# Two of four weight-block sums by an adding transfer in a two-layer decoder trunk

## The chip, the cores and the metric

The kernel runs on one core of one Trainium2 chip. The metric is the device time of one execution, in microseconds. A core has five engines with instruction streams of their own: TensorE (PE; its weight loads are listed as PEld), VectorE (DVE), ScalarE (ACT), GpSimd (POOL) and SyncE (SP), which here only issues transfers.

## The reference

Two decoder layers on 256 tokens of width 2048, in float32. Layer 0 mixes tokens by multi-scale retention, layer 1 by latent attention; each mixer is followed by a SwiGLU block of width 5632, and every sub-layer is normed before and after:

```
for i in range(DEPTH):
    h = rms_norm(x, norm_mix_pre[i])
    h = retention(h, ...) if i % 2 == 0 else mla(h, ...)
    x = x + rms_norm(h, norm_mix_post[i])
    h = rms_norm(x, norm_ffn_pre[i])
    x = x + rms_norm(swiglu(h, ffn_w_gu[i], ffn_w_down[i]), norm_ffn_post[i])

def swiglu(x, w_gu, w_down):
    gate, up = jnp.split(x @ w_gu, [D_FF], axis=-1)
    return (jax.nn.silu(gate) * up) @ w_down
```

## The kernel before

Nearly all time goes into products of the 256 tokens (two tiles t of 128) with large weight matrices. A product is a `group`: it takes one slice of 1024 output columns and runs over the blocks kt of 128 rows of the weights. For each block, `weights` loads 128x1024 float32 from memory on SP's queue into a buffer `raw` (RAW = 4 of them), and `split` makes a high part in a rounded format on ScalarE (line 201) and a low part, the remainder, on VectorE (line 202), each into one of WB = 5 buffers. TensorE multiplies high by high, high by low and low by high: 12 matmuls of 512 columns for each block. `tile_load` issues the loads (line 415).

In some pairs of blocks the product of two by two blocks is made with 7 instead of 8 block products, in Winograd's form (`seven`): pairs p = 2 and 4 in the gate/up groups j = 1 to 10 of each SwiGLU (`GU_SEVENS`), and p = 2, 6, 10, 14, 18 in both halves of each down projection (`DN_SEVENS`). With b00, b01 the two halves of 512 columns of the pair's first block and b10, b11 those of its second, `right_sums` makes four sums of weight blocks:

- t1 = b00 + b01 and t3 = b01 + b11, side by side in the tile ta (lines 244, 245)
- t2 = t1 + b11 and t4 = t2 + b10, side by side in the tile tb (lines 246, 247)

Then ta and tb are split like any weights (tahi, talo, tbhi, tblo), each into one of the same 5 buffers; a pair thus takes 4 of them. ta and tb share 2 buffers (`tsum`). `left_sums` (lines 230 to 233) makes the sums of the activations. The products of a pair go in the order 1, 2, 3, 5, 7, 6, 4, where 5 and 7 read ta, and 6 and 4 read tb; in the last such pair of a group the order is 1, 6, 5, 7, 2, 3, 4, so that tb is read second. The first block of such a pair is loaded whole but only its first half is split (`first_half`); its second half b01 serves the sums alone.

Each engine runs its instructions in the order that a planner of the framework set when the kernel was built. It may put an instruction ahead of one that the program wrote earlier; on the chip an engine then waits at each instruction until its inputs are there, with all that is behind it. SP's transfers go out in order as well: a load waits until the raw buffer that it is to fill has been read by all its readers. The other names in the traces: gu and dn are the gate/up and down projections, m are the banks of products 1, 5, 6 and 7, b those of the result, sf, sh and sl the sums of activations and their parts, rvg, rqk, rto, mc, uq and mlo other products' weights.

Of the kernel before, what the change touches and what calls it, by code (L numbers as in the profile page):

```python
# [12 lines left out]
ALU = mybir.AluOpType  # L13
PSUM = bass.MemoryType.PSUM

P = 128
# [38 lines left out]
def trunk(  # L55
# [19 lines left out]
    nc = tc.nc  # L75
# [5 lines left out]
    def mm_bank(name):  # L81
        return ps.tile([P, 512], F32, tag="mm", bufs=6, name=name)
# [115 lines left out]
    def split(hi, lo, src, g=None):  # L198

        if g is None:  # L200
            nc.scalar.copy(out=hi, in_=src)  # L201
            nc.vector.tensor_sub(out=lo, in0=src, in1=hi.bitcast(F32))  # L202
        else:
            nc.scalar.activation(out=hi, in_=src, func=AF.Copy, scale=g)
            nc.vector.scalar_tensor_tensor(
                out=lo, in0=src, scalar=g, in1=hi.bitcast(F32), op0=ALU.mult, op1=ALU.subtract
            )
# [25 lines left out]
        nc.vector.tensor_add(out=sums[:, 3], in0=sums[:, 1], in1=a01)  # L233
        split(hi, lo, sums)

    def right_sums(raw0, raw1, name):

        b00, b01 = raw0[:, 0:512], raw0[:, 512:1024]
        b10, b11 = raw1[:, 0:512], raw1[:, 512:1024]
        res = {}  # L240
        ta = tp7.tile([P, 1024], F32, tag="tsum", bufs=2, name=f"{name}_ta")
        tb = tp7.tile([P, 1024], F32, tag="tsum", bufs=2, name=f"{name}_tb")
        t1, t3, t2, t4 = ta[:, 0:512], ta[:, 512:1024], tb[:, 0:512], tb[:, 512:1024]
        nc.vector.tensor_add(out=t1, in0=b00, in1=b01)
        nc.vector.tensor_add(out=t3, in0=b01, in1=b11)
        nc.vector.tensor_add(out=t2, in0=t1, in1=b11)
        nc.vector.tensor_add(out=t4, in0=t2, in1=b10)
        for both, src, n in ((ta, (1, 3), "a"), (tb, (2, 4), "b")):
            hi = wp.tile([P, 1024], F32R, tag="whi", bufs=WB, name=f"{name}_t{n}hi")
            lo = wp.tile([P, 1024], F32R, tag="wlo", bufs=WB, name=f"{name}_t{n}lo")  # L250
            split(hi, lo, both)
            for i, k in enumerate(src):
                sl = slice(i * 512, (i + 1) * 512)
                res[k] = hi[:, sl], lo[:, sl]
        return res

    def group(
        lhs, kts, load, name, lead=2, skew=0, tail=0, banks=None, between=None, sevens=(), left=None
    ):

# [5 lines left out]
        if banks is None:  # L266
            banks = [[mm_bank(f"{name}_b{t}{c}") for c in range(2)] for t in range(NT)]
        else:
            cols = banks[1]
            banks = banks[0]  # L270
        w = {}
# [30 lines left out]
            w[kt] = load(kt, True) if kt % 2 == 0 and kt // 2 in sevens else load(kt)  # L302

        def sums(p):
            w["t", p] = right_sums(w[2 * p][2], w[2 * p + 1][2], f"{name}_w{p}")

        def m_banks():
            for i, bank in ((1, mm_bank), (6, mm_bank), (5, misc_bank), (7, misc_bank)):
# [80 lines left out]
        for n, e in enumerate(plan):  # L389
# [15 lines left out]
    def tile_load(w, g, name, halves=0):  # L405

        def load(kt, first_half=False):
            n = 512 if kt < halves or first_half else 1024  # L410

            def dma(raw):
                for a in range(0, 1024, 512 if kt < halves else 1024):
                    m = 512 if kt < halves else 1024
                    nc.sync.dma_start(out=raw[:, a : a + m], in_=w[g, kt, :, a : a + m])

            parts = [(a, n, None) for a in range(0, 512 if first_half else 1024, n)]
            return weights(dma, parts, f"{name}_w{kt}")

        return load  # L420
# [55 lines left out]
    def closing(act, kts, w, g_post, col, name, skew=4, sevens=(), sums=None):  # L476
# [36 lines left out]
        for half in range(2):  # L513
            gp = sb.tile([P, 1024], F32, tag="gp", name=f"{name}_gp")
            nc.sync.dma_start(
                out=gp, in_=g_post[half * 1024 : (half + 1) * 1024].partition_broadcast(P)
# [44 lines left out]
            def first_done(banks):  # L561
# [9 lines left out]
            banks = group(  # L571
                lhs, kts, load, f"{name}{half}", skew=skew if half else 0, tail=2 if half else 0,
                between=first_done if half else None, sevens=sevens,
                left=lambda p, half=half: parts["s", half, p],
            )
            if half:
                stats(banks, 1)
# [191 lines left out]
    def swiglu(i):  # L769
        with tc.tile_pool(name=f"ff{i}", bufs=1) as fp:  # L770
# [32 lines left out]
            for j in range(FF // 512):  # L803
                name = f"gu{i}_{j}"
                banks = group(
                    h_lhs, DT, tile_load(w_gu[i], j, name), name, lead=2 if j else 4,
                    sevens=GU_SEVENS if 0 < j else (), left=lambda p: ins[p],
                )
# [289 lines left out]
    swiglu(0)  # L1098
    mla()
    swiglu(1)  # L1100


# [89 lines left out]
```

## Time and profile before

| what | value |
|---|---|
| median of 3 runs | 2454.28 us (2453.28 to 2454.59) |
| profiled execution, its time | 2454.15 us |
| its span, first to last instruction | 2452.3 us |
| busy: PE / PEld / DVE / ACT / POOL | 99% / 83% / 73% / 53% / 1% |
| moved by transfers | 463.75 MB, 189 GB/s |
| share of the 16 DMA engines, SP's queue | 57.1% |
| mean granted TensorE clock | 0.999 |

A row of the timeline gives start, duration, engine, line, operation, output<-inputs, shape and, in brackets, how long the engine was idle before it and what ended that. A row of groups gives the count, then busy microseconds and the mean nanoseconds of one, then the idle time before them with its releasers. A name that ends in q, as SPq, is an engine's queue of issues. Some hundredths of a microsecond between a releaser's end and the start of what it releases are normal. A low or high half in the text is the low or high part of a split, not half a block's columns.

### The profile page before, as it was taken

How to read it: one execution, taken by the hardware profiler on the slowest of the kernel's cores; microseconds unless marked ns; L12 is line 12 of the kernel's file. 1: busy time of each engine (PE TensorE's matmuls, PEld its weight loads, DVE VectorE, ACT ScalarE, POOL GpSimd, SP SyncE). 2: the span in 40 equal slices, each digit the busy share in tenths (PEclk: the TensorE clock that was granted, in tenths of full speed). 3: DMA queues.
4: the chain of work that ended last, by engine and by line, in shares of the span. 5: the costliest groups of instructions: out<-in, count | busy, mean ns of one | idle time of the engine just before them, and what ended most of it. 6: DMA issues, size and time to landing. Idle time of an engine off the chain costs nothing.

```text
span 2452.3 us, 30456 instructions
## 1 busy us (share of the span) xinstructions
PE 2438.9 (99%) x11128; PEld 2023.6 (83%) x11128; DVE 1799.4 (73%) x2379; ACT 1311.1 (53%) x1751; POOL 27.1 (1%) x38
## 2 busy tenths in 40 slices
PE   9999999999999999999999999999999999999998
PEld 7888888888888888888888888888888888888887
DVE  7655555555657787787888887876778777788887
ACT  5434544445545554555556666655555554556664
POOL 0000000000000000000000000000000000000000
PEclk9999999999999999999999999999999999999999
DMA  7555555555565566565656655445556656565664
GB/s 261 186 185 178 182 181 181 180 181 181 198 197 189 172 211 200 182 212 180 207 181 210 208 198 162 129 134 193 188 174 210 197 185 211 187 200 183 214 204 155
DMA packets 129607, 463.75 MB, mean 189 GB/s; under 512 B 14640, under 2 KB 15024, under 8 KB 129456
## 3 DMA queue, kind: packets, MB, share of 16 engines
q1 hardware_dynamic: 129456, 461.80, 57.1%
q8 instruction: 87, 1.43, 0.2%
q14 instruction: 64, 0.52, 0.1%
HBM read 459.64 MB, written 2.10 MB: 188 GB/s over the span
## 4 chain that ended last, share of the span: by engine, by line
PE 99%; DMA 0%; DVE 0%; SPq 0%; ACT 0%; issue 0%; DVEq 0%; POOL 0%; POOLq 0%; ACTq 0%
PE gu_b L398 34%; PE dn_b L398 17%; PE rvg_b L398 14%; PE rto_b L398 7%; PE rqk_b L398 7%; PE gu_m L398 4%; PE mlo_b L398 4%; PE q L398 3%; PE dn_m L398 2%; PE mc_b L398 2%; PE ftp L776 1%; PE ry L721 1%; PE htp L434 1%; PE asc L1032 0%; PE rsc L676 0%; PE asc L1029 0%
## 5 line engine op out<-in xcount | busy, mean ns | idle before, releaser
L398 PE MATMUL gu_b<-gu_w_hi,hT 128*128 128x512 f32 x2256 | 640.8, 392 | 0.0
L201 ACT CAST gu_w_hi<-gu_w_raw 128x1024 fp32r<-128x1024 f32 (+1 forms) x352 | 349.4, 1003 | 327.7 <-PE gu_b L398 252.3
L202 DVE TENSOR_TENSOR gu_w_lo<-gu_w_raw,gu_w_hi 128x1024 fp32r<-128x1024 f32 (+1 forms) x352 | 402.7, 1159 | 120.3 <-ACT gu_w_hi L201 120.0
L398 PEld LDWEIGHTS gu_b<-gu_w_hi,hT 128*128 128x128 f32 x2256 | 419.4, 188 | 85.7 <-DVE hT L202 0.9
L398 PE MATMUL gu_b<-gu_w_lo,hT 128*128 128x512 f32 x1128 | 358.2, 390 | 0.0
L398 PE MATMUL rvg_b<-rvg_w_hi,hT 128*128 128x512 f32 x1024 | 280.8, 391 | 0.0
L202 DVE TENSOR_TENSOR rvg_w_lo<-rvg_w_raw,rvg_w_hi 128x1024 fp32r<-128x1024 f32 x128 | 156.4, 1224 | 160.6 <-ACT rvg_w_hi L201 160.6
L398 PEld LDWEIGHTS gu_b<-gu_w_lo,hT 128*128 128x128 f32 x1128 | 211.5, 188 | 44.8 <-DVE gu_w_lo L202 0.6
L201 ACT CAST rvg_w_hi<-rvg_w_raw 128x1024 fp32r<-128x1024 f32 x128 | 134.7, 1053 | 195.8 <-PE rvg_b L398 187.4
L201 ACT CAST dn_w_hi<-dn_w_raw 128x1024 fp32r<-128x1024 f32 (+1 forms) x176 | 174.3, 1003 | 104.1 <-PE dn_b L398 55.9
L398 PEld LDWEIGHTS rvg_b<-rvg_w_hi,hT 128*128 128x128 f32 x1024 | 191.1, 188 | 38.9
L202 DVE TENSOR_TENSOR dn_w_lo<-dn_w_raw,dn_w_hi 128x1024 fp32r<-128x1024 f32 (+1 forms) x176 | 200.0, 1160 | 23.6 <-ACT dn_w_hi L201 22.9
L398 PE MATMUL dn_b<-dn_w_hi,dn_ah 128*128 128x512 f32 x564 | 178.2, 390 | 0.0
L398 PE MATMUL dn_b<-dn_w_lo,dn_ah 128*128 128x512 f32 x564 | 178.0, 390 | 0.0
L398 PE MATMUL dn_b<-dn_w_hi,dn_al 128*128 128x512 f32 x564 | 178.0, 390 | 0.0
L398 PE MATMUL rvg_b<-rvg_w_lo,hT 128*128 128x512 f32 x512 | 158.1, 390 | 0.0
L398 PE MATMUL rqk_b<-rqk_w_hi,hT 128*128 128x512 f32 x512 | 141.0, 393 | 2.0 <-ACT hT L201 1.0
L398 PEld LDWEIGHTS dn_b<-dn_w_lo,dn_ah 128*128 128x128 f32 x564 | 105.9, 188 | 22.0
L398 PEld LDWEIGHTS dn_b<-dn_w_hi,dn_al 128*128 128x128 f32 x564 | 105.9, 188 | 21.9
L398 PEld LDWEIGHTS dn_b<-dn_w_hi,dn_ah 128*128 128x128 f32 x564 | 105.6, 188 | 21.6
L202 DVE TENSOR_TENSOR rqk_w_lo<-rqk_w_raw,rqk_w_hi 128x1024 fp32r<-128x1024 f32 (+1 forms) x65 | 77.5, 1207 | 59.3 <-ACT rqk_w_hi L201 59.3
L201 ACT CAST rqk_w_hi<-rqk_w_raw 128x1024 fp32r<-128x1024 f32 (+1 forms) x65 | 67.4, 1038 | 99.4 <-PE rqk_b L398 90.2
(307 smaller groups left out, 3851.6 us busy)
## 6 DMA issues: line engine op xcount, KB each, us to landing
gu_w_raw<-w_gu SPq DMA_DIRECT2D x352, 512.0 KB, 4.3
dn_w_raw<-w_down SPq DMA_DIRECT2D x176, 512.0 KB, 4.4
rvg_w_raw<-ret_vg SPq DMA_DIRECT2D x128, 512.0 KB, 3.5
rto_w_raw<-ret_out SPq DMA_DIRECT2D x64, 512.0 KB, 3.5
rqk_w_raw<-ret_qk SPq DMA_DIRECT2D x63, 512.0 KB, 4.0
mlo_w_raw<-mla_out SPq DMA_DIRECT2D x32, 512.0 KB, 3.5
uq_w_raw<-mla_up SPq DMA_DIRECT2D x32, 448.0 KB, 3.4
mc_w_raw<-mla_c SPq DMA_DIRECT2D x16, 512.0 KB, 4.6
```

The source lines that it names most:

```text
L201: nc.scalar.copy(out=hi, in_=src)
L202: nc.vector.tensor_sub(out=lo, in0=src, in1=hi.bitcast(F32))
L398: nc.tensor.matmul(out, e[2](), e[3](), start=bank not in begun, stop=ends[bank, bank in added] == n, skip_group_check=bank in added,)
L434: nc.tensor.transpose(tp[:, j * P : (j + 1) * P], xs[:, t, (k0 + j) * P : (k0 + j + 1) * P], ident)
L721: nc.tensor.matmul(y, left, right, start=n == 0, stop=n == len(terms) - 1)
L776: nc.tensor.transpose(tp[:, b * P : (b + 1) * P], a[:, b * P : (b + 1) * P], ident)
```

## The change

Of a pair's first block only the first half is loaded into its raw buffer. ScalarE copies b00 into t1's place and b11 into t3's place in ta. Then one transfer, issued by GpSimd, reads b01 from memory twice (a source repeated over two rows) and adds it to both halves of ta. t2 and t4 stay adds on VectorE.

```
-        nc.vector.tensor_add(out=t1, in0=b00, in1=b01)
-        nc.vector.tensor_add(out=t3, in0=b01, in1=b11)
+        nc.scalar.copy(out=t1, in_=b00)
+        nc.scalar.copy(out=t3, in_=b11)
+        nc.gpsimd.dma_start(
+            out=ta.rearrange("p (i c) -> p i c", i=2),
+            in_=b01_again[:, None, :].to_broadcast([P, 2, 512]), accum_op=ALU.add,
+        )
         nc.vector.tensor_add(out=t2, in0=t1, in1=b11)
         nc.vector.tensor_add(out=t4, in0=t2, in1=b10)
...
-                for a in range(0, 1024, 512 if kt < halves else 1024):
-                    m = 512 if kt < halves else 1024
-                    nc.sync.dma_start(out=raw[:, a : a + m], in_=w[g, kt, :, a : a + m])
+                for a in range(0, 512 if first_half else 1024, n):
+                    nc.sync.dma_start(out=raw[:, a : a + n], in_=w[g, kt, :, a : a + n])
```

The argument `b01_again` is the slice `[..., 512:1024]` of the weights in memory, handed down through a new parameter `second_half` of `group`; in the down projection it is `w[half, kt, :, 512:1024]`, in gate/up `w_gu[i][j, kt, :, 512:1024]`.

More of the change, by code (lines that the diff above doesn't have):

```diff
@@ L234, in left_sums, with right_sums @@
         split(hi, lo, sums)
-    def right_sums(raw0, raw1, name):
-        b00, b01 = raw0[:, 0:512], raw0[:, 512:1024]
+    def right_sums(raw0, raw1, b01_again, name):
+        b00 = raw0[:, 0:512]
         b10, b11 = raw1[:, 0:512], raw1[:, 512:1024]
@@ L257, in group @@
     def group(
-        lhs, kts, load, name, lead=2, skew=0, tail=0, banks=None, between=None, sevens=(), left=None
+        lhs, kts, load, name, lead=2, skew=0, tail=0, banks=None, between=None, sevens=(), left=None,
+        second_half=None,
     ):
@@ L304, in sums @@
         def sums(p):
-            w["t", p] = right_sums(w[2 * p][2], w[2 * p + 1][2], f"{name}_w{p}")
+            w["t", p] = right_sums(w[2 * p][2], w[2 * p + 1][2], second_half(2 * p), f"{name}_w{p}")
         def m_banks():
@@ L574, in closing @@
                 left=lambda p, half=half: parts["s", half, p],
+                second_half=lambda kt, half=half: w[half, kt, :, 512:1024],
             )
@@ L807, in swiglu @@
                     sevens=GU_SEVENS if 0 < j else (), left=lambda p: ins[p],
+                    second_half=lambda kt, j=j: w_gu[i][j, kt, :, 512:1024],
                 )
```

## The prediction

> **What bounds the kernel now.** I read the page's busy times first, then the chain that ended last, then a window over everything but the first 12 us and the last ones. The first row is the page's, the second its chain, the third the window (length, then busy time and count of PE, PEld, DVE, ACT, POOL, then granted clock, DMA share, GB/s).
>
> ```profile
> PE 2438.9 (99%) x11128; PEld 2023.6 (83%) x11128; DVE 1799.4 (73%) x2379; ACT 1311.1 (53%) x1751; POOL 27.1 (1%) x38
> ...
> PE 99%; DMA 0%; DVE 0%; SPq 0%; ACT 0%; issue 0%; DVEq 0%; POOL 0%; POOLq 0%; ACTq 0%
> ...
> 12.00:2440.00 2428.00, 2427.32 (x11084) 2016.98 (x11083) 1788.07 (x2356) 1303.04 (x1731) 26.31 (x33) 1.00 0.57 189
> ```
>
> TensorE is the bound and nothing else is: in 2428.00 us it is idle for 0.68 us, at full clock. VectorE's 1788 us in that window lie wholly beside it. So work taken off VectorE can give at most 0.68 us; the change alters no matrix product, so it can only leave the time alone or cost time. Everything turns on whether the sums of weight blocks still arrive before TensorE asks for them.
>
> **The change part by part.** It touches right_sums, which runs 60 times: 40 times in the gate/up groups and 20 times in the down projection. The adds that go:
>
> ```profile
> L245 DVE TENSOR_TENSOR gu_w_ta<-gu_w_raw 128x512 f32<-128x512 f32 x40 | 27.6, 690 | 32.2 <-DMA gu_w_raw<-w_gu 32.2
> L244 DVE TENSOR_TENSOR gu_w_ta<-gu_w_raw 128x512 f32<-128x512 f32 x40 | 27.6, 690 | 4.7 <-DMA gu_w_raw<-w_gu 4.0
> L245 DVE TENSOR_TENSOR dn_w_ta<-dn_w_raw 128x512 f32<-128x512 f32 x20 | 13.7, 686 | 0.0
> L244 DVE TENSOR_TENSOR dn_w_ta<-dn_w_raw 128x512 f32<-128x512 f32 x20 | 13.7, 685 | 0.0
> ...
> L777 ACT COPY aT<-ftp 128x512 f32<-128x512 f32 x44 | 25.5, 579 | 0.0
> ```
>
> Removed from VectorE: 27.6 + 27.6 + 13.7 + 13.7 = 82.6 us, worth nothing by the window above. Added on ScalarE: 2 copies of 128x512 in each of 60 places at the 0.579 us of the last row (that one reads PSUM; it is the nearest), 120 x 0.579 = 69.5 us, hidden under its idle 47% as long as they are not late themselves.
>
> Added as transfers: 60 on GpSimd's queue, each writing 512 KB and reading 256 KB of weights twice; 60 loads on SP's queue shrink from 512 to 256 KB. Net 60 x 256 KB = 15.7 MB on the 463.75 MB of the page, 3.4%. The page's first row counts 38 instructions on GpSimd in the whole kernel, so next to nothing queues behind the new wait there. SP's queue is another matter, below.
>
> The price that no row shows is L: from the end of the second copy to the landed sum. The nearest rows are SP's plain loads (KB, then median us from issue to landing) and GpSimd's small operations (count, busy us, mean ns):
>
> ```profile
> gu_w_raw<-w_gu SPq DMA_DIRECT2D x352, 512.0 KB, 4.3
> dn_w_raw<-w_down SPq DMA_DIRECT2D x176, 512.0 KB, 4.4
> ...
> cst<-consts SPq DMA_DIRECT2D x1, 64.0 KB, 1.9
> ...
> L118 POOL TENSOR_TENSOR grs<-bve,mhalf 128x1 f32<-128x1 f32 x16 | 8.8, 548 | 550.8 <-DVE bve L727 550.8
> L118 POOL TENSOR_TENSOR rto_x_r<-rto_x_v,mhalf 128x1 f32<-128x1 f32 x2 | 4.2, 2096 | 24.0 <-DVE rto_x_s L451 23.7 <-DVE rto_x_v L453 0.3
> ```
>
> Lower end: 4.3 us, if the transfer costs what a plain load of its size does. Upper end: it must also read its 512 KB target before it can add, and GpSimd issues it instead of SP; two loads in a row and the longest GpSimd row give 2 x 4.3 + 2.1 = 10.7 us. Between: the 64 KB row puts the part that does not grow at about 1.9 us, so 512 KB move in 2.4 us; twice that, plus 1.9, plus 0.55 for GpSimd, is 6.85. The GpSimd part is nearer to its 0.55 than to 2.1, but the new transfer also shares 16 engines that are busy 57% of the time, so I take L = 7.2 us, an estimate.
>
> The Trainium skill bears on the doubling: "Collectives: The Full Stack", section "The bandwidth ceiling", says that a transfer that adds sends two reads for each chunk through the same ring and so runs at half the rate of a copy. No row here shows an adding transfer; by that rule alone the sum would be the one I take.
>
> Now where L lies. These are the rows of one gate/up group's two sums (block pairs 2 and 4), VectorE first, then TensorE:
>
> ```profile
> 929.24 0.68 DVE L245 TENSOR_TENSOR gu_w_ta<-gu_w_raw 128x512 f32<-128x512 f32 x1
> ...
> 933.81 1.23 DVE L202 TENSOR_TENSOR gu_w_lo<-gu_w_raw,gu_w_hi 128x1024 fp32r<-128x1024 f32 x1 [1.29 <-ACT gu_w_hi L201]
> ...
> 938.50 0.69 DVE L245 TENSOR_TENSOR gu_w_ta<-gu_w_raw 128x512 f32<-128x512 f32 x1 [1.33 <-DMA gu_w_raw<-w_gu]
> 939.11 1.22 DVE L202 TENSOR_TENSOR gu_w_tblo<-gu_w_tb,gu_w_tbhi 128x1024 fp32r<-128x1024 f32 x1
> ...
> 940.45 0.68 DVE L246 TENSOR_TENSOR gu_w_tb<-gu_w_ta,gu_w_raw 128x512 f32<-128x512 f32 x1
> ...
> 941.25 0.68 DVE L247 TENSOR_TENSOR gu_w_tb<-gu_w_tb,gu_w_raw 128x512 f32<-128x512 f32 x1
> 941.85 2.95 DVE L202 TENSOR_TENSOR gu_w_lo<-gu_w_raw,gu_w_hi 128x1024 fp32r<-128x1024 f32 x3
> ...
> 947.95 1.05 ACT L201 CAST gu_w_tbhi<-gu_w_tb 128x1024 fp32r<-128x1024 f32 x1 [1.66 <-PE gu_b L398]
> ...
> 949.03 1.23 DVE L202 TENSOR_TENSOR gu_w_tblo<-gu_w_tb,gu_w_tbhi 128x1024 fp32r<-128x1024 f32 x1 [1.49 <-ACT gu_w_tbhi L201]
> ...
> 943.90 0.39 PE L398 MATMUL gu_m<-gu_w_tblo,sh 128*128 128x512 f32 x1
> 945.49 0.39 PE L398 MATMUL gu_b<-gu_w_lo,hT 128*128 128x512 f32 x1
> ...
> 951.38 0.39 PE L398 MATMUL gu_m<-gu_w_tblo,sh 128*128 128x512 f32 x1
> ```
>
> After the landed transfer, the rest of the chain is two adds (941.25 + 0.68 - 940.45 = 1.48 us), the high half on ScalarE (1.05) and the low half on VectorE (1.22): 3.75 us.
>
> First sum of the group: its second block is there at 929.24. Copy 0.58, L, 3.75: the low half is ready at 933.57 + L, and TensorE reads it at 943.90. Hidden up to L = 10.3.
>
> Second sum: hidden cover is shorter, because the first one now delays its load. The raw buffer of the first sum's second block was freed by the low half that ends at 933.81 + 1.23 = 935.04. Now the two late adds read that buffer too, and end at 929.24 + 0.58 + L + 1.48 = 931.30 + L. With 4 raw buffers, the load four blocks on (the second block of the second sum, landed at 938.50) waits for just this buffer, on SP's in-order queue, as it did before:
>
> ```profile
> SPq L415 <- DVE gu_w_lo L202: 789.7, 341, 8.1
> ```
>
> It therefore lands L - 3.74 later, at 934.76 + L. Copy 0.58, L again, 3.75: ready at 939.09 + 2L, wanted at 951.38. It is in time up to L = 6.14; beyond that TensorE stops for 2L - 12.29. At L = 7.2 that is 2.1 us, in 20 groups (10 of each layer's 11) 42 us.
>
> In the down projection two sums are further apart, and the load four blocks on is no sum's. An ordinary place and the last of a half:
>
> ```profile
> 2234.49 0.69 DVE L245 TENSOR_TENSOR dn_w_ta<-dn_w_raw 128x512 f32<-128x512 f32 x1
> 2246.55 0.39 PE L398 MATMUL dn_m<-dn_w_tblo,sh 128*128 128x512 f32 x1
> ...
> 2297.61 0.69 DVE L245 TENSOR_TENSOR dn_w_ta<-dn_w_raw 128x512 f32<-128x512 f32 x1
> ...
> 2307.07 0.39 PE L398 MATMUL dn_m<-dn_w_tblo,sh 128*128 128x512 f32 x1
> ```
>
> Ordinary: 12.06 - 0.58 - 3.75, hidden up to 7.7. Last: 9.46 - 4.33, hidden up to 5.1, so 2.1 us at L = 7.2, four times (two halves, two layers): 8 us.
>
> Sum: 42 + 8 = 50 us on the profiled execution's own 2454.15 us, which stands 0.1 us under the median of the runs: 2504 us. At 8.6 (two loads in a row) it is 20 x 4.9 + 4 x 3.5 + 16 x 0.9 = 126 us, 2580; at 10.7 about 2700; at 4.3 nothing.
>
> **The rivals.**
> Hidden anyway (the other side: not slower). If L stays under 5.1 us every sum is in time by the above, and 2454 us stays; between 5.1 and 6.1 only the four last sums are late, at most 4 us in all. For it: the plain loads' 4.3 us. Against it: the second read and GpSimd's part. The Trainium skill, "DMA: Bandwidth & Descriptors", section "Anatomy of one DMA", gives about 2.0 us plus bytes over 436 GB/s for a transfer issued by GpSimd; with 512 KB that is 3.2 us and with the target's read counted too 4.4 us, both estimates, and by either the time stays 2454 us. No run here shows it yet.
>
> The order on VectorE. Its instructions start in a planned order, not when they are ready. The row at 939.11 shows it: its high half was long cast, and it stood behind the add that waited 1.33 us for a load. If the plan puts the add that needs the transfer (as now, 940.45) ahead of the three low halves of 941.85, they stand behind it. TensorE reads the first of them at 945.49. At L = 4.3 the load lands 0.56 us later, the transfer at 939.06 + 0.58 + 4.3 = 943.94, two adds and one low half end at 946.64: 1.15 us late, 23 us over 20 groups, 2477 us, although L itself would be hidden. At 7.2 it is 1.15 + 2 x 2.9 = 6.95 us, 139 us, 2593. Against it: a plan that reckons with a late transfer sets those halves first.
>
> A transfer much slower than two loads (over 8.6 us): beyond 2580 us. Only the upper end of L speaks for it.
>
> **How the numbers follow.** Forecast, L between 6.1 and 8.6 with the order adapted: 0.36. Hidden: 0.34. Order: 0.19. Slower transfer: 0.09. Faster: 0.02, since the window leaves 0.68 us and 0.2% (5 us, about what a measurement tells from no change) is needed. Same gets the hidden case and the forecast's edge, 0.35; slower 0.63. The likeliest case gives 2504 us, with its own range 2459 to 2580. The range 2453 to 2600 takes in the hidden case at one end and most of the order's at the other; the slower transfer and the rest of the order's case, about 0.15, lie outside.
>
> **What would show it.** Right: VectorE's busy time falls by about 80 us, ScalarE's rises by about 70, and TensorE has gaps of some 2 us, 20 of them at the product that reads the gate/up sums' second pair and 4 at the down projection's last, released by VectorE's low half or ScalarE's high half of tb; the transfers take about 7 us from issue to landing. Wrong by size: landing in 5 us or less and TensorE still without gaps. Wrong by place: gaps at the ordinary low halves, with VectorE idle in front of the add that makes t2.

## The result and the profile after

The changed kernel takes 2671.71 us (median of 4, 2665.79 to 2676.48) beside 2454.41 us for the kernel before on the same chip: a ratio of 1.0885, 95% interval 1.0862 to 1.0908, 217 us more. The prediction had the sign and the place of the gate/up stops; it gave 2504 us, 50 us more, with a range to 2600, so the loss is four times the forecast and outside the range.

The page of the changed kernel: busy times, chain, GpSimd's queue (packets, MB, share of 16 engines' span) and its two groups of transfers (count, KB each, median us from issue to landing).

```profile
PE 2536.1 (95%) x11128; PEld 2063.5 (77%) x11128; DVE 1723.8 (64%) x2259; ACT 1360.4 (51%) x1871; POOL 100.1 (4%) x98
...
q0 software_dynamic: 16320, 31.46, 7.3%
...
PE 62%; DMA 19%; DVE 10%; issue 4%; ACT 4%; SPq 0%; DVEq 0%; ACTq 0%; POOL 0%; POOLq 0%
...
gu_w_ta<-w_gu POOLq DMA_DIRECT2D x40, 512.0 KB, 6.4
dn_w_ta<-w_down POOLq DMA_DIRECT2D x20, 512.0 KB, 9.3
```

A chain that was 99% TensorE is now 62%, with 19% transfers and 10% VectorE. VectorE's 75.6 us less and ScalarE's 49.3 us more go the way of the moved work (the copies' records overlap their neighbours', so their 120 x 0.62 us do not add up in full). The loss is in the first row: the span grew by 222.1 us (2452.3 to 2674.4); TensorE's idle time grew from 13.4 to 138.3 us, and its busy time by 97.2 us for the same 11128 matmuls. These are two losses of different kinds.

The idle time, by groups (idle before them and its releaser last in the row):

```profile
L405 PE MATMUL gu_m<-gu_w_tbhi,sh 128*128 128x512 f32 x40 | 18.7, 467 | 43.1 <-ACT gu_w_tbhi L201 43.1
L405 PE MATMUL gu_m<-gu_w_tblo,sh 128*128 128x512 f32 x40 | 21.6, 541 | 16.7 <-DVE gu_w_tblo L202 16.7
L405 PE MATMUL dn_b<-dn_w_lo,dn_ah 128*128 128x512 f32 x564 | 182.1, 397 | 32.9 <-DVE dn_w_lo L202 32.9
L405 PE MATMUL dn_m<-dn_w_tbhi,sh 128*128 128x512 f32 x20 | 9.9, 496 | 15.9 <-ACT dn_w_tbhi L201 15.9
L405 PE MATMUL dn_m<-dn_w_tblo,sh 128*128 128x512 f32 x20 | 10.5, 527 | 5.5 <-DVE dn_w_tblo L202 5.5
L405 PE MATMUL dn_m<-dn_w_talo,sh 128*128 128x512 f32 x40 | 22.2, 556 | 4.8 <-DVE dn_w_talo L202 4.8
```

Gate/up stops almost only where a product reads tb (43.1 + 16.7 = 59.8 us; 3.8 us stand at ordinary low halves). In the down projection a little more than half, 32.9 us, stands at ordinary low halves, which are made from no sum; the last three rows, 26.2 us, are products that read sums.

The busy time, by windows over the two gate/up stages (first and third row) and the two down projections (length, then PE, PEld, DVE, ACT, POOL busy and count, granted clock, DMA share, GB/s); the last row is a stretch of 3.3 us right after one gate/up stop:

```profile
753.00:1291.00 538.00, 506.31 (x2159) 408.10 (x2157) 358.11 (x420) 275.75 (x347) 29.10 (x23) 0.96 0.61 184
1291.00:1575.00 284.00, 252.90 (x1038) 201.38 (x1037) 183.85 (x238) 148.65 (x212) 12.70 (x11) 0.94 0.59 175
1845.00:2386.00 541.00, 507.02 (x2160) 406.65 (x2159) 357.75 (x418) 276.91 (x345) 29.31 (x24) 0.96 0.61 184
2386.00:2668.00 282.00, 250.60 (x1024) 199.37 (x1022) 181.01 (x231) 142.27 (x190) 12.71 (x12) 0.94 0.56 166
...
1020.80:1024.10 3.30, 3.30 (x9) 2.52 (x9) 2.63 (x3) 0.79 (x1) 0.00 (x0) 0.50 0.49 178
```

The granted clock, 1.00 before, is 0.96 and 0.94: after most stops it is 0.50 for 3.4 or 6.8 us. Summed over the four stages that is 160 us at half clock, so up to 80 us of the 97.2 (the matmuls that began at half clock make up some 70 us of it). Most of the rest are the first matmuls behind a stop: they count with their whole record, where in a stream the records overlap.

One gate/up group, its two sums, in order of time:

```profile
995.29 0.62 ACT L246 COPY gu_w_ta<-gu_w_raw 128x512 f32<-128x512 f32 x1
...
1002.14 0.69 DVE L251 TENSOR_TENSOR gu_w_tb<-gu_w_ta,gu_w_raw 128x512 f32<-128x512 f32 x1 [5.87 <-DMA gu_w_ta<-w_gu]
1002.75 1.22 DVE L202 TENSOR_TENSOR gu_w_lo<-gu_w_raw,gu_w_hi 128x1024 fp32r<-128x1024 f32 x1
1003.88 0.69 DVE L252 TENSOR_TENSOR gu_w_tb<-gu_w_tb,gu_w_raw 128x512 f32<-128x512 f32 x1
...
1008.13 0.62 ACT L246 COPY gu_w_ta<-gu_w_raw 128x512 f32<-128x512 f32 x1 [0.34 <-DMA gu_w_raw<-w_gu]
1009.16 1.20 POOL L247 DMA_DIRECT2D gu_w_ta<-w_gu  x1 [11.62 <-ACT gu_w_ta L246]
1015.63 0.69 DVE L251 TENSOR_TENSOR gu_w_tb<-gu_w_ta,gu_w_raw 128x512 f32<-128x512 f32 x1 [2.93 <-issue]
1016.24 1.22 DVE L202 TENSOR_TENSOR gu_w_lo<-gu_w_raw,gu_w_hi 128x1024 fp32r<-128x1024 f32 x1
1017.37 0.69 DVE L252 TENSOR_TENSOR gu_w_tb<-gu_w_tb,gu_w_raw 128x512 f32<-128x512 f32 x1
...
1018.17 1.05 ACT L201 CAST gu_w_tbhi<-gu_w_tb 128x1024 fp32r<-128x1024 f32 x1 [1.46 <-DVE gu_w_tb L252]
1019.24 1.23 DVE L202 TENSOR_TENSOR gu_w_tblo<-gu_w_tb,gu_w_tbhi 128x1024 fp32r<-128x1024 f32 x1
1019.26 0.50 PE L405 MATMUL gu_m<-gu_w_tbhi,sh 128*128 128x512 f32 x1 [2.17 <-ACT gu_w_tbhi L201]
1020.52 0.60 PE L405 MATMUL gu_m<-gu_w_tblo,sh 128*128 128x512 f32 x1 [0.76 <-DVE gu_w_tblo L202]
```

From the start of the last copy to t2 the first sum takes 6.85 us, the second 7.50; a low half (the second and the fifth VectorE row) stands between t2 and t4 in both. (The L of the tables below counts from GpSimd's issue, which begins some 0.4 us after the copy's end: 995.91 to 996.33 in this group.) Between the two sums lies a load that lands 3.5 us after the first t4 ends. SP's queue waited for those adds; its waits (total us, times, longest):

```profile
SPq L421 <- DVE gu_w_tb L252: 254.6, 38, 9.8
...
SPq L421 <- DVE dn_w_tb L252: 203.0, 20, 11.8
```

In the kernel before, the same two waits are next to nothing:

```profile
SPq L415 <- DVE dn_w_tb L247: 5.1, 2, 2.6
...
SPq L415 <- DVE gu_w_tb L247: 0.8, 1, 0.8
```

An ordinary place of the down projection:

```profile
1378.29 0.69 DVE L251 TENSOR_TENSOR dn_w_tb<-dn_w_ta,dn_w_raw 128x512 f32<-128x512 f32 x1 [8.01 <-DMA dn_w_ta<-w_down]
1378.90 1.22 DVE L202 TENSOR_TENSOR dn_w_lo<-dn_w_raw,dn_w_hi 128x1024 fp32r<-128x1024 f32 x1
...
1380.17 0.80 PE L405 MATMUL dn_b<-dn_w_lo,dn_ah 128*128 128x512 f32 x1 [3.23 <-DVE dn_w_lo L202]
```

VectorE waits 8.01 us at t2 for the transfer; behind it stands a low half that needs nothing of the sum, and TensorE needs that half.

### The profile page after: what moved, and what is told of

Its sections match the earlier page's. It is cut to its first block, busy times and chain, and to the rows that moved or that the text cites. A ratio compares the mean times of both kernels' runs of the same rounds, so it can differ in the third digit from the quotient of the medians.

```text
span 2674.4 us, 30714 instructions
## 1 busy us (share of the span) xinstructions
PE 2536.1 (95%) x11128; PEld 2063.5 (77%) x11128; DVE 1723.8 (64%) x2259; ACT 1360.4 (51%) x1871; POOL 100.1 (4%) x98
## 4 chain that ended last, share of the span: by engine, by line
PE 62%; DMA 19%; DVE 10%; issue 4%; ACT 4%; SPq 0%; DVEq 0%; ACTq 0%; POOL 0%; POOLq 0%
PE gu_b L405 18%; PE rvg_b L405 13%; DMA gu_w_ta<-w_gu 8%; PE rto_b L405 7%; PE rqk_b L405 6%; DMA dn_w_ta<-w_down 6%; PE mlo_b L405 3%; PE dn_b L405 3%; PE q L405 3%; DMA dn_w_raw<-w_down 3%; PE gu_m L405 3%; DVE dn_w_lo L202 2%; DMA gu_w_raw<-w_gu 2%; DVE gu_w_lo L202 2%; PE mc_b L405 2%
## 5 line engine op out<-in xcount | busy, mean ns | idle before, releaser
L201 ACT CAST gu_w_hi<-gu_w_raw 128x1024 fp32r<-128x1024 f32 (+1 forms) x352 | 343.0, 1001 | 285.5 <-PE gu_b L405 226.1
L405 PE MATMUL dn_b<-dn_w_lo,dn_ah 128*128 128x512 f32 x564 | 182.1, 397 | 32.9 <-DVE dn_w_lo L202 32.9
L251 DVE TENSOR_TENSOR gu_w_tb<-gu_w_ta,gu_w_raw 128x512 f32<-128x512 f32 x40 | 27.7, 693 | 184.2 <-DMA gu_w_ta<-w_gu 139.3
```

The source lines that it names most:

```text
L405: nc.tensor.matmul(out, e[2](), e[3](), start=bank not in begun, stop=ends[bank, bank in added] == n, skip_group_check=bank in added,)
```

## The experiments

In the table, the times are medians in us, each beside the kernel before on the same chip; the stages are the spans of the two gate/up stages and the two down projections in the profiled run; L is the median us from issue to landing of the transfers in gate/up and in the down projection.

| kernel | time | ratio, 95% interval | gate/up | down | L |
|---|---|---|---|---|---|
| before | 2454.4 | | 478.2, 478.2 | 234.3, 233.3 | |
| after | 2671.71 | 1.0885 (1.0862 to 1.0908) | 538.6, 541.0 | 284.1, 282.5 | 6.4, 9.3 |
| filled stop | 2633.26 | 1.0738 (1.0704 to 1.0772) | 521.0, 521.9 | 280.8, 281.2 | 6.2, 9.1 |
| no wait | 2459.30 | 1.0024 (1.0014 to 1.0033) | 480.8, 479.9 | 234.4, 233.3 | 7.0, 9.8 |
| t2, t4 on GpSimd | 2727.28 | 1.1115 (1.1098 to 1.1131) | 554.3, 564.2 | 288.6, 289.4 | 6.4, 9.0 |
| half the transfer | 2492.57 | 1.0157 (1.0142 to 1.0172) | 486.4, 486.9 | 248.6, 240.8 | 4.4, 7.2 |
| t2 behind the low half | 2718.52 | 1.1085 (1.1060 to 1.1109) | 572.0, 568.3 | 275.6, 272.3 | 8.1, 9.1 |
| writing, by GpSimd | 2516.15 | 1.0253 (1.0229 to 1.0277) | 484.4, 484.9 | 255.7, 253.5 | 4.5, 6.2 |
| writing, by ScalarE | 2503.37 | 1.0201 (1.0184 to 1.0218) | 494.4, 499.4 | 239.7, 240.1 | 4.5, 6.1 |
| five raw buffers | 2670.99 | 1.0878 (1.0860 to 1.0895) | 545.5, 551.6 | 270.8, 272.7 | 7.2, 9.5 |
| gate/up pairs 2 and 5 | 2662.27 | 1.0842 (1.0827 to 1.0857) | 540.3, 536.0 | 280.8, 277.4 | 6.8, 8.9 |
| second sum only | 2557.09 | 1.0417 (1.0401 to 1.0433) | 480.8, 479.4 | 283.8, 280.6 | 6.4, 9.2 |
| first sum only | 2617.19 | 1.0668 (1.0638 to 1.0697) | 518.8, 513.5 | 285.1, 281.6 | 8.0, 9.2 |
| split behind t4 | 2672.39 | 1.0877 (1.0859 to 1.0895) | 542.5, 533.5 | 285.1, 282.8 | 6.4, 9.3 |

The theories by their letters: A, the half clock is caused by the stops; B, the wait costs and not the added work; C, VectorE's order makes the down projection's stops; D, the length L sets the stops; E, adding is dearer than writing; F, the first sum holds its raw buffer and so delays the second; G, what adding costs when nothing shares the engines; H, the low half between t2 and t4.

**A, the clock.** Twelve matmuls of zeros fill the stop in front of product 6 of a group's last pair:

```
+    FILL = 12
...
+                if final and i == 6:
+                    plan.append(("do", fill))
                 product(*m[i])
...
+        def fill():
+            for _ in range(FILL):
+                nc.tensor.matmul(ms[6], zeros, zeros[:, None, :].to_broadcast([P, 4, P]), start=False, stop=False)
```

> The changed kernel with 12 matmuls of zeros (about 0.22 us each) put ahead of product 6 of the last pair of each group, so that TensorE works while it waits for tb. Theory A: a part of the loss is TensorE's clock, which the profile of the changed kernel shows at 0.5 for 3.4 or 6.8 us behind each longer stop (47.8 and 44.4 us in the two gate/up stages, of which half is lost: 46 us). With TensorE kept busy the half-clock stretches in gate/up go, the stop stays as long as the zero matmuls: about 2672 - 46 = 2626 us. Rival: the clock record costs nothing, or follows something else than the stop: the time stays within 8 us of the changed kernel's 2672.

The first gate/up stage of that kernel:

```profile
753.00:1274.00 521.00, 512.32 (x2281) 403.90 (x2280) 359.01 (x421) 276.95 (x347) 29.09 (x23) 1.00 0.63 190
```

The clock is 1.00 and the stages are 17.6 and 19.1 us shorter, although TensorE waits for the same sums. So this part of the loss comes after the stop, not in it. Of the 46 us that gate/up had lost to half clock 37 came back; the rest the added matmuls may have cost.

**B, the wait.** All the copies and transfers stay but write into an array that is unused at the time (yg), while VectorE makes t1 and t3 as before:

```
+        side = yg_box[0][:, 1, 1024:2048]
+        nc.scalar.copy(out=side[:, 0:512], in_=b00)
...
+        nc.vector.tensor_add(out=t1, in0=b00, in1=b01)
+        nc.vector.tensor_add(out=t3, in0=b01, in1=b11)
         nc.gpsimd.dma_start(
-            out=ta.rearrange("p (i c) -> p i c", i=2),
+            out=side.rearrange("p (i c) -> p i c", i=2),
```

> All the work of the change without the wait: VectorE makes t1 and t3 as before (the first block is loaded whole again), and beside it ScalarE makes its two copies and GpSimd's queue its adding transfer, into a stretch of yg that nobody reads at that time. Theory B (it is the wait for the transfer): the time of the kernel before, 2454 us, within 6 us. Rival (the traffic, GpSimd's issuing or ScalarE's copies disturb the loads or the other engines): over 2470 us, with loads that land later than 4.3 us.

The transfers are no shorter (7.0 and 9.8 us), but no sum waits for them: work and traffic are worth 4.9 us of the 217. VectorE keeps its adds here, and the first blocks are loaded whole, so that the traffic is rather more than in the change. The rest is waiting and what follows from it.

**C, VectorE's order.** Two ways to take t2 out of the low half's way. First t2 and t4 on GpSimd:

```
-        nc.vector.tensor_add(out=t2, in0=t1, in1=b11)
-        nc.vector.tensor_add(out=t4, in0=t2, in1=b10)
+        nc.gpsimd.tensor_add(out=t2, in0=t1, in1=b11)
+        nc.gpsimd.tensor_add(out=t4, in0=t2, in1=b10)
```

> The changed kernel with t2 and t4 added by GpSimd instead of VectorE, so that no instruction of VectorE's queue waits for the transfer ahead of a low half. Theory C (order: low halves stand behind the add that waits): the gaps at the down projection's ordinary low halves, 12 of them with 35 us idle and some 15 us of half clock behind them, vanish, and in gate/up the low half between t2 and t4 no longer holds t4 up (2 x 1.1 us in 20 groups); GpSimd's adds are slower by an unknown amount, at 1.3 us more a pair some 50 us are given back: about 2620 us. Rival (the transfer's length alone): the gaps stay, the slower adds come on top, 2680 us or more.

The stop at the down projection's low halves is gone (32.9 us to 0.0 in the same group of the table of groups), but the whole got slower: GpSimd's adds take 1286 and 2145 ns each in gate/up, where VectorE's took 0.69 us, and the time comes back at the products that read the sums. The theory's place held, its total did not. Second, t2 queued behind the low half of the pair's second block:

```
-        nc.vector.tensor_add(out=t2, in0=t1, in1=b11)
+        with tc.issue_after(last_lo[0].ins):
+            nc.vector.tensor_add(out=t2, in0=t1, in1=b11)
```

> The changed kernel with one order fixed: on VectorE's queue the add that makes t2, which waits for the transfer, is put behind the low half of the pair's second block instead of ahead of it; nothing else. Theory C again, without slower adds: the down projection's gaps at ordinary low halves (12, 35 us idle, and the half clock behind them) vanish, and in gate/up t4 follows t2 at once, 1.1 us sooner in both sums of 20 groups (45 us idle, and a part of its 46 us of half clock): 2540 to 2600 us. Rival (only the transfer's length counts, the gaps reappear at the products that read tb): over 2640 us.

```profile
L407 PE MATMUL dn_b<-dn_w_lo,dn_ah 128*128 128x512 f32 x564 | 179.4, 392 | 0.0
...
L407 PE MATMUL gu_m<-gu_w_tbhi,sh 128*128 128x512 f32 x40 | 23.7, 592 | 119.2 <-ACT gu_w_tbhi L202 119.2
```

In the down projection the stop at the low half vanished and the stages fell by 8.5 and 10.2 us, less than the stop itself: products that read ta now waited 18.3 and 11.9 us for its low and high halves (4.8 and 1.5 in the changed kernel). In gate/up the planner, given one more rule, put other work in another order too, L rose to 8.1 us, and the stop at tb grew from 43.1 to 119.2 us. The total is a miss; it tells of the down projection only.

**D, the length.** The transfer adds to t1 alone, so that t3 lacks b01:

```
-            out=ta.rearrange("p (i c) -> p i c", i=2),
-            in_=b01_again[:, None, :].to_broadcast([P, 2, 512]), accum_op=ALU.add,
+            out=t1, in_=b01_again, accum_op=ALU.add,
```

> The changed kernel with a transfer of half the size: b01 is added to t1 alone (t3 is left as b11 alone, so that sum is left out). Theory D (the transfer's length, and in it the bytes): it lands 2 us sooner in gate/up (6.4 to about 4.4 us from issue) and 3 us sooner in the down projection (9.3 to about 6.3), the gate/up stops vanish nearly (2 x 2 us against 3) and the down projection's get shorter: 2490 to 2530 us. Rival (a fixed cost of issue and landing, or the order): landing less than 0.7 us sooner, over 2630 us.

L falls by 2 us and four fifths of the loss go, as expected. L is a main term of the loss, and a steep one.

**E, adding or issuing.** The same transfer writes instead of adding, on GpSimd's queue and then on ScalarE's (in both t1 and t3 are then b01 itself):

```
-            in_=b01_again[:, None, :].to_broadcast([P, 2, 512]), accum_op=ALU.add,
+            in_=b01_again[:, None, :].to_broadcast([P, 2, 512]),
...
-        nc.gpsimd.dma_start(
+        nc.scalar.dma_start(
```

> The changed kernel with the same transfer from the same queue, waits and all, but writing b01 twice instead of adding it (t1 and t3 are then b01, so that part of the sum is left out). Theory E (adding costs the target's read, as the prediction had it): landing about 1.3 us sooner in gate/up (6.4 to about 5.1 us) and more in the down projection, and a time of 2540 to 2600 us. Rival (what takes long is GpSimd's issuing, 1.2 us, the start, 0.8 us, and the sharing of the engines with SP's loads): landing within 0.4 us of the changed kernel's, time over 2640 us.

> As the run with the writing transfer, but issued on ScalarE's queue instead of GpSimd's (which can't add; t1 and t3 are again b01). Theory E: the issue by GpSimd costs some 1.5 us more than one by ScalarE, so the transfer lands in about 3.8 us from issue in gate/up and the stops there vanish; the time is 30 to 80 us under that of the GpSimd one. Rival (who issues does not matter, the bytes do): landing within 0.5 us of the GpSimd one, time within 15 us of it.

The transfers of the one and of the other:

```profile
gu_w_ta<-w_gu POOLq DMA_DIRECT2D x40, 512.0 KB, 4.5
```

```profile
gu_w_ta<-w_gu ACTq DMA_DIRECT2D x40, 512.0 KB, 4.5
```

Adding costs 1.9 us here (6.4 against 4.5) and 3.1 in the down projection, more than expected, and the writing transfer's 2516 us lie below the 2540 expected. Who issues makes no difference to the landing, so the issuer's theory failed and its rival held. The stages do differ, though: with ScalarE's queue gate/up is 10.0 and 14.5 us longer and the down projection 16.0 and 13.4 us shorter at the same L. Nor is the down projection of the writing transfer by GpSimd (L 6.2 us) shorter than that of the half transfer (7.2 us): 255.7 and 253.5 us against 248.6 and 240.8. L alone does not set a stage's time; what else does was not looked for.

**G, alone.** Behind the end of the kernel before, six transfers of each kind, each kind one after the other: adding (tl_t), writing by GpSimd (tl_u), a plain load by SP (tl_v).

```
+        for k in range(6):
+            nc.gpsimd.dma_start(
+                out=t.rearrange("p (i c) -> p i c", i=2),
+                in_=src[:, None, :].to_broadcast([P, 2, 512]), accum_op=ALU.add,
+            )
...
+        for k in range(6):
+            nc.gpsimd.dma_start(
+                out=u.rearrange("p (i c) -> p i c", i=2),
+                in_=src[:, None, :].to_broadcast([P, 2, 512]),
+            )
...
+        for k in range(6):
+            nc.sync.dma_start(out=v, in_=w_gu[0][1, 4])
```

> The kernel before with 18 transfers of 512 KB behind its end, one after the other, with nothing else in flight: 6 adding ones as in the change, 6 writing ones of the same shape from GpSimd, 6 plain loads from SP (their targets are read by nobody). It prices the transfer by itself. Theory G (the length in the kernel is GpSimd's issue, the added read and the sharing of the engines with SP's loads): the adding one lands in about 4.8 us alone, against a median of 6.4 in gate/up and 9.3 in the down projection, the writing one in about 4, SP's in about 3.4. Rival (adding is slow by itself): 6 us or more alone. The time is about 2454 + 6 x (4.8 + 4 + 3.4) + some 10 = 2540 us.

```profile
tl_t<-w_gu POOLq DMA_DIRECT2D x6, 512.0 KB, 6.5
tl_u<-w_gu POOLq DMA_DIRECT2D x6, 512.0 KB, 4.3
tl_v<-w_gu SPq DMA_DIRECT2D x6, 512.0 KB, 3.5
```

Adding takes 6.5 us alone, not the 4.8 expected: the rival held. (This is one run, 2531.89 us. The planner began the first four adding transfers beside the end of the kernel's own work; all six took 6.3 to 6.6 us.) So gate/up's 6.4 us is about the bare price of adding, and the down projection's 9.3 is 2.8 us above it. That does not rule out contention in gate/up: in three other kernels the same transfer takes 7.2 to 8.1 us there, and in the group shown above the three loads issued beside the second transfer (1011.0 to 1012.7 us) took 6.2 to 7.0 us, the four issued before the first 3.2 to 4.4.

**F, the held buffer.** Two tests that changed other things as well. A fifth raw buffer, paid for by one buffer less of ah and al:

```
-    RAW, WB = 4, 5
+    RAW, WB = 5, 5
```

> The changed kernel with 5 raw buffers instead of 4 (room is made by 2 instead of 3 buffers for the activations' parts in the closings, so only the gate/up stages are read). Theory F (the first sum's late adds hold the buffer that the second sum's load needs): the load no longer waits, the second sum's copy starts some 2 us sooner in each of 20 groups (then held by the buffers of ta), and the two gate/up stages, 538.6 and 541.0 us long with the change, get 2 x (10 x 2) = 40 us or more shorter together. Rival (the load was not what set the second sum's time): the stages stay within 8 us.

And the two sums of a gate/up group set further apart:

```
-GU_SEVENS = (2, 4)
+GU_SEVENS = (2, 5)
```

> The changed kernel with the gate/up pairs 2 and 5 instead of 2 and 4, so that the load four blocks behind the first sum's second block belongs to no sum. Theory F again (the first sum's late adds hold the raw buffer and so make the second sum late): the second sum's copy and transfer are no longer late, the stops at its products shrink from 3 us to under 1 us in 20 groups and the half clock behind them goes: the gate/up stages fall from 538.6 and 541.0 us to about 490 to 500 each, 2580 to 2600 us in all. Rival (the second sum is late by its own transfer and order): the stages stay above 525 us.

Neither made a gate/up stage shorter by more than 5 us. With five buffers the stops moved from tb to ordinary low halves (82.6 us there). SP's queue waited 0.8 us in all for t4 (254.6 in the changed kernel), but the load for the second sum still left late, in all 20 groups right behind a low half that VectorE ran after t2:

```profile
1001.86 0.69 DVE L251 TENSOR_TENSOR gu_w_tb<-gu_w_ta,gu_w_raw 128x512 f32<-128x512 f32 x1 [5.86 <-DMA gu_w_ta<-w_gu]
...
1003.13 0.68 DVE L202 TENSOR_TENSOR gu_w_lo<-gu_w_raw,gu_w_hi 128x512 fp32r<-128x512 f32 x1
...
1003.84 0.33 SPq L421 DMA_DIRECT2D gu_w_raw<-w_gu  x1
```

That is 2.0 us after the first transfer landed, where the changed kernel's load left 2.5 us after it (at 1004.63, behind t4's end at 1004.57, in the group above). The fifth buffer passed the hold from t4 to another instruction behind the same wait. With the pairs apart SP's queue still waited 213.8 us for t4 in 20 places, and loads behind the held one queue in order. Both are misses of the theory as it was put, and left open whether F or the low half between t2 and t4 was the cause. The next three were run for that. The transfer for the second sum of each gate/up group only, and then for the first only (sevens[0] in place of sevens[-1]); the other sum is made by VectorE from a whole load:

```
+        if whole:
+            nc.vector.tensor_add(out=t1, in0=b00, in1=raw0[:, 512:1024])
+            nc.vector.tensor_add(out=t3, in0=raw0[:, 512:1024], in1=b11)
+        else:
             nc.scalar.copy(out=t1, in_=b00)
...
+        def old(p):
+            return len(sevens) == 2 and p != sevens[-1]
```

> The transfer makes t1 and t3 only for the second sum of each gate/up group (block pair 4); the first sum of the group (pair 2) is made by two adds on VectorE from a whole load, as before the change. The down projection stays as changed. Theory F (the first sum's late adds hold its raw buffer, which delays the load that the second sum needs): with the first sum on time that load lands as before, at about 938.5 on the walk of before, and with L = 6.8 the second sum's low half is ready at about 949.7 for a use at 951.4, so the gate/up stages come back to within 10 us of before (478 us, where both changed sums give 538.6 and 541.0) and their half clock goes to nearly nothing; whole about 2555. Rival (order: a low half of 1.13 us and the adds behind the wait make the second sum late whatever the first did): the gate/up stages stay over 515 us and the gaps stay at the products that read tb.

The two gate/up stages of that kernel, and its group that reads tbhi:

```profile
753.00:1233.00 480.00, 478.28 (x2157) 394.39 (x2157) 367.88 (x440) 270.84 (x327) 16.99 (x13) 1.00 0.63 200
...
1785.00:2263.00 478.00, 477.49 (x2155) 394.10 (x2154) 367.66 (x439) 271.74 (x328) 16.74 (x13) 1.00 0.63 201
```

```profile
L415 PE MATMUL gu_m<-gu_w_tbhi,sh 128*128 128x512 f32 x40 | 15.6, 389 | 0.0
```

The same second transfer, with the same 6.4 us, is hidden to 2.6 and 1.2 us of a stage once the first sum is on time. So the second sum is late because the first one is, as F has it. That the delay goes by the held buffer and the late load is read from the walks and from SP's waits.

> The mirror image: the transfer makes t1 and t3 only for the first sum of each gate/up group (pair 2), the second (pair 4) is made on VectorE from a whole load. The down projection stays as changed. Theory F: the first sum has slack (hidden up to L = 10.3), and the second has only the load's delay of L - 3.7 = 3.1 us and no transfer behind it, ready at about 945.6 for a use at 951.4: gate/up stages within 10 us of before, whole about 2555. Rival (each such sum costs its own share through VectorE's order): about half of the loss stays, gate/up stages 505 to 515 us.

The second sum of a group of that kernel, made on VectorE:

```profile
1931.06 0.69 DVE L248 TENSOR_TENSOR gu_w_ta<-gu_w_raw 128x512 f32<-128x512 f32 x1 [0.74 <-DMA gu_w_raw<-w_gu]
1931.66 0.69 DVE L256 TENSOR_TENSOR gu_w_tb<-gu_w_ta,gu_w_raw 128x512 f32<-128x512 f32 x1
...
1933.47 2.95 DVE L202 TENSOR_TENSOR gu_w_lo<-gu_w_raw,gu_w_hi 128x1024 fp32r<-128x1024 f32 x3
...
1934.74 1.20 PE L415 MATMUL gu_b<-gu_w_lo,hT 128*128 128x512 f32 x2 [2.50 <-DVE gu_w_lo L202]
```

The first sum alone costs 40.6 and 35.3 us, more than half of what both cost, though the second has no transfer. In the group shown the load for it left at 1927.38 us, right behind the first sum's t4, and landed at 1931.03: it is late, and the adds for it stand on VectorE ahead of the three low halves that TensorE needs next. My expectation of under 10 us had left that queue out; the rival's number came true by the first sum's hold, not by a share of each sum. The number is no exact share of the changed kernel's loss either, since the transfer itself took 8.0 us here, not 6.4.

**H, the low half in between.** The split of the pair's second block queued behind t4:

```
-        nc.vector.tensor_add(out=t4, in0=t2, in1=b10)
+        t4_add = nc.vector.tensor_add(out=t4, in0=t2, in1=b10)
+        with tc.issue_after(t4_add.ins):
+            split(k1[0], k1[1], raw1)
```

> The changed kernel, with the split of each seven-product pair's second block (one high and one low half) queued behind the add that makes t4, so that this low half no longer stands between t2 and t4. Theory H (order within the sum): the gate/up stop, 1.3 us by 2L - 12.29 at L = 6.8 plus 2 x 1.13 us for that low half in both sums, falls by 2.26 us in each of 40 groups of two layers' 20 (45 us less idle and some of the half clock with it): gate/up stages 500 to 515 us each, whole 2580 to 2620. Rival (F alone: the raw buffer held by the first sum sets the second): no more than 10 us in the two stages, or longer, since that low half now comes later to its own product and frees the raw buffer later.

```profile
2106.40 0.69 DVE L253 TENSOR_TENSOR gu_w_tb<-gu_w_ta,gu_w_raw 128x512 f32<-128x512 f32 x1 [2.90 <-issue]
2107.13 0.69 DVE L254 TENSOR_TENSOR gu_w_tb<-gu_w_tb,gu_w_raw 128x512 f32<-128x512 f32 x1
...
2110.01 1.22 DVE L202 TENSOR_TENSOR gu_w_tblo<-gu_w_tb,gu_w_tbhi 128x1024 fp32r<-128x1024 f32 x1
```

Nothing changed. t4 now follows t2 at once, but the low half only moved behind it and still stands ahead of tblo: t2's start to tblo's end is 4.83 us here (2106.40 to 2111.23) and 4.84 in the changed kernel (1015.63 to 1020.47). The expectation had counted as removed what was only moved. What those halves cost is therefore read from the walk, not shown by a kernel.

**Two kernels beside the question.** Both are the kernel before with one edit: t1 and t3 as adds on GpSimd (which takes the same adds off VectorE without a transfer), and a sixth pair of seven products in the down projection.

```
-        nc.vector.tensor_add(out=t1, in0=b00, in1=b01)
-        nc.vector.tensor_add(out=t3, in0=b01, in1=b11)
+        nc.gpsimd.tensor_add(out=t1, in0=b00, in1=b01)
+        nc.gpsimd.tensor_add(out=t3, in0=b01, in1=b11)
```

> The kernel before with t1 and t3 added by GpSimd instead of VectorE, no copies and no transfer. Another way to take the same 82.6 us off VectorE. By the rows of GpSimd's adds in an earlier run (1.29 and 2.15 us) t1 and t3 together take 3.4 us in place of 1.4, 2 us later than before, where the last sum of a group has 1.1 us to spare: some 1 us in each of 24 places, 2465 to 2490 us, far under the changed kernel. Rival (any wait for another engine ahead of t2 costs as the transfer does): over 2550 us.

2454.21 us, ratio 0.9999 (0.9990 to 1.0008): 120 adds at 1.5 to 1.9 us each are hidden, better than expected. But VectorE was not relieved. It has 120 adds fewer, yet the page's first row and the group of t2's add, 687 ns each in the kernel before, read:

```profile
PE 2440.2 (100%) x11128; PEld 2024.2 (83%) x11128; DVE 1803.5 (74%) x2259; ACT 1311.5 (53%) x1751; POOL 223.5 (9%) x158
...
L246 DVE TENSOR_TENSOR gu_w_tb<-gu_w_ta,gu_w_raw 128x512 f32<-128x512 f32 x40 | 58.3, 1457 | 4.8 <-DMA gu_w_raw<-w_gu 3.2 <-DVE gu_w_tblo L202 0.4
```

VectorE's 1803.5 us are 4.1 more than before: instructions of VectorE's that meet GpSimd's adds are longer. One add of t2 took 1.45 us (at 929.97) beside a GpSimd add that ran to 930.87, the next one 0.68 (at 941.58), when GpSimd's add had ended.

```
-DN_SEVENS = (2, 6, 10, 14, 18)
+DN_SEVENS = (2, 5, 8, 11, 14, 18)
```

> The kernel before with six seven-product pairs in each half of the down projection (2, 5, 8, 11, 14, 18) instead of five: 3 matmuls of 0.227 us fewer in each of 4 halves, for some 6.4 us more of VectorE's time in each. If TensorE's count is all that bounds, 2.7 us less than before, 0.11%. Rival: VectorE's queue is too full there and the sums come late, 3 us or more longer.

2451.88 us, ratio 0.9989 (0.9980 to 0.9998): 2.6 us less, 2.7 expected. It is the one version here whose interval lies below the kernel before, by 0.1%; it takes matmuls away, 11116 instead of 11128.

## Why the prediction was right in kind and wrong in size

**Right: the bound and the sign.** With TensorE idle for 0.68 us in the window before there was next to nothing to gain, and the changed kernel, with 75.6 us less on VectorE, is slower; what was added cost 4.9 us as work (B) and all else by waiting and what follows from it. No kernel here relieves VectorE without adding a wait: the one with t1 and t3 on GpSimd left its busy time where it was.

**Right: the mechanism in gate/up; its stops came to 60 us for 42.** The prediction's chain, late adds, a held raw buffer, a late load, a second late sum, is what the walk and SP's queue show, and F's pair of kernels shows that it begins at the first sum. Its formula 2L - 12.29 can be filled in from the walk. Without the copy's 0.58 the two sums took L = 6.27 and 6.92: 13.19 - 12.29 = 0.90 us, less than the 2.1 taken. But where it let t2 and t4 follow each other (1.48 us) and tblo come after 3.75 us, they took 2.43 (1002.14 to 1004.57) and 4.84: an ordinary low half stood between t2 and t4 on VectorE, which is most of the 0.95 + 1.09 = 2.04 us. Together 2.94 us; the stop was 2.17 + 0.76 = 2.93. Over 20 groups like this one that is 59 us where 42 were forecast, and the groups show 59.8. L was taken too long (1.2 us too much for each stop), and the queue was left out of the very walk whose rows showed it (2.0 us too little). The two errors go against each other: that 42 comes so near is in part luck.

**Failed: no term for the clock.** "At L = 7.2 that is 2.1 us, in 20 groups (10 of each layer's 11) 42 us" priced a stop at its own length. Most stops of 2 to 3 us also halved the clock for 3.4 or 6.8 us: up to 80 us in all, more than the whole forecast of 50. In all the gate/up stages lost 60.4 and 62.8 us, twice their stops. Experiment A shows the cause for gate/up: with the stop filled the clock stays at 1.00. The Trainium skill, "TensorE: Matmul & The Clock Gate", section "HAM oscillation — how this bites in real kernels", describes this loss after waits for data, with the rule that idle gaps should stay under about 3.4 us. Its 3.4 us come back here as the length of a stretch at half clock, once or twice over; as a limit for the gaps they do not hold. Stops of 2.17 and 0.76 us, with one matmul in between, were enough, and in the kernel with the first sum only a single stop of 2.50 us was: the row below is the stretch behind it, its granted clock third from the end.

```profile
1934.90:1938.20 3.30, 3.30 (x8) 2.65 (x9) 3.30 (x7) 0.00 (x0) 0.00 (x0) 0.50 0.65 204
```

Nor is there a sharp limit in these traces. In the changed kernel 19 of the 20 stops in gate/up were followed by half clock; in its down projection one stop of 2.52 us was (at 2613.84 us), another of 2.52 us was not (at 1496.52). Every price of a stop in the prediction, the rivals' too, lacks this term.

**Failed: the down projection.** Forecast 8 us, measured 49.8 + 49.2 = 99. Two steps of it failed. L was one number for all; it is 6.4 in gate/up and 9.3 here, beyond the 7.7 to which ordinary places were hidden. With 9.3 the prediction's own sum would have been 16 x 1.6 + 4 x 4.2 = 42 us, an estimate. And the rival of VectorE's order was priced for gate/up alone, and given 0.19; it came true in the down projection, at 12 ordinary low halves, in just the form named under "wrong by place": VectorE idle in front of t2 (8.01 us) and TensorE stopped at a low half. Experiment C removed those stops by queuing t2 behind, but the stages stayed 41.3 and 39.0 us above the kernel before: the order is worth some 10 us of each stage's 50; the rest goes with the late transfer and the clock. 34 of the 99 us were lost to half clock; most of the rest is in the groups shown, 32.9 us at these halves and 26.2 at products that read sums. That L grows because SP's loads share the engines is likely (512 KB alone take 6.5), but no kernel here removed the loads.

**The price of adding.** The two-reads estimate, 6.85 us, is near the 6.5 measured alone, and its part for the second read, 2.4 us, near the 2.2 by which adding exceeds writing (6.5 against 4.3). The rival "hidden anyway" rested on a short price and is refuted by the 6.5. The Trainium skill, "DMA: Bandwidth & Descriptors", section "Anatomy of one DMA", gave estimates of 3.2 us, or 4.4 with the target's read; the writing transfer's 4.3 us and the adding one's 6.5 exceed them. "Slower transfer" (over 8.6) was true for the down projection and was given 0.09 as a case of its own; the cases were not exclusive, and two of them came at once there, which the range did not provide for.

## What to carry to other kernels

Where one engine is busy 99% of the time, a result that comes late costs three things: the stop, the half clock after it, and whatever stands behind the waiting instruction in its engine's queue; price all three, for every place, before counting what the moved work saves. Follow a late result through the buffers that it holds: here the second sum's transfer was harmless (2.6 us of a stage) as long as the first sum was on time, and the first one's, which held a load's buffer, cost 40.6 us by itself. An idle engine's slower add, hidden at 1.5 to 1.9 us, cost no time where a transfer of 6.4 us did; but it did not unload VectorE, whose busy time stayed, so look at both engines' rows before calling such a move a relief.

## What the hardware showed that I had not expected

- Most stops of 2 to 3 us are followed by a granted clock of 0.50 for 3.4 or 6.8 us (19 of 20 in gate/up).
- An adding transfer of 512 KB takes 6.5 us alone, a writing one 4.3, a plain load 3.5; GpSimd's issue takes 1.2 us for the one and 0.73 for the other. ScalarE's queue lands a writing transfer no sooner than GpSimd's (4.5 us).
- Beside the down projection's loads the adding transfer takes 9.3 us. The median of all those loads stays at 4.3 (4.4 before), but loads issued beside a transfer can take longer: 6.2 to 7.0 us for three of them in the gate/up group shown.
- GpSimd's adds of 128x512 float32 take 1.3 to 2.1 us where VectorE's take 0.69, and VectorE's own adds are longer beside them (t2's: 1457 ns on average, 687 before).
